# Three edits to a two-layer hybrid decoder trunk: a late weight part used later, two gated products on GpSimd, one low part first

## The chip, the cores and the metric

One core of one Trainium2 chip runs the whole program. The metric is the time of one execution in device microseconds (us); the figure of record is the median of the runs. Engines are named as the profile names them: PE is TensorE's matmul part and PEld its weight load, DVE is VectorE, ACT is ScalarE, POOL is GpSimd, SP is SyncE, whose queue issues nearly all DMAs.

## The reference, cut to what matters

Sequence 1024, model width 1024, everything float32. Layer 0 mixes with a gated linear recurrence, layer 1 with sliding-window attention; each layer then has a gated feed-forward block, and after each sub-layer stands a layer norm of `alpha * x + sublayer(x)`.

```python
def hgrn2_mixer(h, w_in, lower_bound, g_norm_w, w_out):      # layer 0
    q, f, i, g = jnp.split(h @ w_in, 4, axis=-1)
    ...
    o = hgrn2_chunkwise(jax.nn.silu(heads(q)), 1.0 - fg, heads(i), jnp.log(fg))
    o = o * lax.rsqrt(jnp.mean(jnp.square(o), -1, keepdims=True) + RMS_EPS)
    o = o * g_norm_w.astype(jnp.float32) * jax.nn.silu(heads(g))
    return o.reshape(B, S, D).astype(h.dtype) @ w_out
...
    o = jnp.einsum('bngrts,bnsgd->bntgrd', p, vv.astype(jnp.float32))   # layer 1
    o = o / jnp.moveaxis(denom, -1, 2)[..., None]
    return o.reshape(B, S, D).astype(h.dtype) @ w_out
...
def conv_ffn(h, w_in, conv_w, conv_b, w_out):                # both layers
    u = h @ w_in                                             # 1024 -> 2 x 2816
    u = lax.conv_general_dilated(u, ...) + conv_b            # causal, width 3
    a, b = jnp.split(u, 2, axis=-1)
    return (jax.nn.silu(a) * b) @ w_out
```

## The kernel before, in words

**Two parts of every number.** The large products are not done in plain float32. Each operand is kept as a high part (a cast to fp32r by ScalarE, the copy in `split`, line 221, or in `split_into`, line 176) and a low part (what is left, a VectorE subtraction in `low_part`, line 169). `mm3` (lines 193 to 197) then issues three matmuls: high by high (194), high by low (195) and low by high (196). So a block of activations (tile T) or of weights (HL, HT, TX) is ready for all three only when VectorE's subtraction is done, behind ScalarE's cast. `low_part` either issues the subtraction at once or, when it is given a list, puts a function there that issues it later.

**The order of the work.** Matmuls stand on PE in the order of the program text. In the recurrence and the attention the order on ACT, DVE and POOL is written out as well; there, a small planner (class `Order`) lets chains of work take turns at each `od.tick()`. In the feed-forward block (`Up`, `Down`) the order on ACT, DVE, POOL and SP is chosen by the compiler layer's scheduler, so one moved instruction can reorder its neighbours. Each engine carries out its own queue strictly in order, and so does SP's queue of DMA issues.

**Place 1, the beginning of layer 0's output projection (lines 1256 to 1274).** Seven of the eight heads' outputs are in T, and the last head's recurrence is still going on. Four accumulators of 128 tokens by 512 columns (`psmm`, one PSUM bank each) are begun: for each block `tb`, seven matmuls of T's high part by the weights' high part (`w` = 0), then seven by the weights' low part (`w` = 1), line 1263. After all four, line 1272 adds T's low part by the weights' high part. The weights `us[0]` to `us[6]` come from four weight units; the last unit holds `us[6]` (and `us[7]`), and its low part is the last one that VectorE makes. The planner sets matmuls of the last head's recurrence (`mm32`, line 200, and transposes, line 204) between them.

**Place 2, the up-projection's beginning, in both layers (`Up.run`, `Up.collect`).** A unit `fc` is 128 of the 2816 hidden columns, with both branches. Its product is put together from seven products of half size, `p` = 1 to 7, each 12 matmuls of 512 columns into one of eight PSUM banks (`psmm` and `psax`); `collect` adds the banks into rows of Y on DVE (lines 454 to 465). At `p` = 4 (first branch) and `p` = 3 (second branch) the width-3 convolution follows: one ACT operation (471) and two DVE operations (473); the first branch then has SiLU on ACT (476). The second branch's result is always in row 6 of Y; line 478 multiplies the two branches into row 4 or 5, and line 479 stores the row to DRAM (`gd`), to be read in the down-projection. Units 0 and 1 are made together and unit after unit from there. Beside this, `weight_sums` makes the next units' weights: sums and differences on DVE (425 to 428) and splits (ACT line 221, DVE line 169).

**Place 3, the attention's end (lines 1486 to 1517 and the lines after the loop).** Pairs of blocks (`bp`) of a head column `c` go through the stages of `attend`: scores and a copy of them (ACT 1410), bias and mask (POOL 1422), the row's extreme and exponential (DVE 1426, ACT 1429), normalisation (DVE 1432, 1433), transposes into a `psmm` bank (PE 204), products with a triangular mask (DVE 1441), and the product with the values into another `psmm` bank (`po`). For the last column, `c` = 7, the result is split straight out of PSUM into T (line 1457); its low part goes to the list `lows`, which `make_lows` empties from the front. In the loop's last turn the list holds already the low part of a move of finished columns from Y to T (`Y_to_T`). There are four `psmm` banks; at this point two of them hold accumulators of the output projection, and transposes and `po` share the other two.

Of the kernel before, what the change touches and what calls it, by code (L numbers as in the profile page):

```python
# [14 lines left out]
ALU = mybir.AluOpType  # L15

P = 128
# [90 lines left out]
def trunk(ctx: ExitStack, tc: tile.TileContext, a: dict, out: bass.AP):  # L108
# [240 lines left out]
    class Up:  # L349
# [97 lines left out]
        def collect(self, p, fc, ps):  # L447
            l, C = self.l, Y[:, 2 * (fc % 2):2 * (fc % 2) + 2, :]
            C11, C21, C12, C22 = C[:, 0, :512], C[:, 0, 512:], C[:, 1, :512], C[:, 1, 512:]
            if p == 1:  # L450
                nc.scalar.copy(C11, ps)
                nc.scalar.copy(C12, ps)
            elif p == 2:
                tt(C11, C11, ps, op=add)
            elif p == 6:
                tt(C12, C12, ps, op=add)
            elif p == 7:
                tt(C22, C12, ps, op=add)
            elif p == 4:
                tt(C21, C22, ps, op=add)  # L460
            elif p == 5:
                both = C[:, 1, :].rearrange("p (h n) -> p h n", h=2)
                tt(both, both, ps.unsqueeze(1).to_broadcast([P, 2, 512]), op=add)
            elif p == 3:
                tt(C12, C12, ps, op=add)
            if p in (4, 3):
                part = 0 if p == 4 else 1
                ci = fc + part * NF
                u, ca = C[:, part, :], Y[:, 4 + fc % 2, :]
                c = Y[:, 6, :] if part else ca  # L470
                nc.scalar.activation(c, u, AF.Identity, bias=cwt[:, l, 3, ci:ci + 1], scale=cwt[:, l, 2, ci:ci + 1])  # L471
                for sh in (1, 2):
                    nc.vector.scalar_tensor_tensor(c[:, sh:], u[:, :S - sh], cwt[:, l, 2 - sh, ci:ci + 1],  # L473
                                                   c[:, sh:], op0=ALU.mult, op1=ALU.add)
                if part == 0:
                    nc.scalar.activation(c, c, AF.Silu)
                else:
                    tt(ca, ca, c, op=ALU.mult)
                    nc.sync.dma_start(gd[:, fc, :], ca)

        def run(self, ready, down):
# [171 lines left out]
    with tc.tile_pool(name="t", bufs=1, reuse_waits="tile") as raws, hgrn_pool as hp:  # L653
# [538 lines left out]
        with tc.manual_schedule(engines={EN.PE, EN.SP, EN.Activation, EN.DVE, EN.Pool}):  # L1192
# [62 lines left out]
            moved.append(od.spawn(moves(NB // 2 - 1), 3.0))  # L1255
            us = out_us
            begun = []
            for tb in range(4):
                begun.append(psmm())
                ts = slice(tb * P, (tb + 1) * P)  # L1260
                for w in range(2):
                    for kc in range(KC - 1):
                        nc.tensor.matmul(begun[tb], T[:, 0, kc, ts], us[kc][:, w, :], start=w + kc == 0, stop=False)
                        od.t += 512 / 2365.0
                        od.tick()
            for tb in range(4):
                ts = slice(tb * P, (tb + 1) * P)
                movelows.sort(key=lambda m: m[0])
                while movelows and movelows[0][0] <= tb // 2:
                    lay_moved()  # L1270
                for kc in range(KC - 1):
                    nc.tensor.matmul(begun[tb], T[:, 1, kc, ts], us[kc][:, 0, :], start=False, stop=False)
                    od.t += 512 / 2365.0
                    od.tick()
            while values_done[0] < NH - 1:
                od.step(task)
            od.finish(moved)
# [30 lines left out]
    with (tc.tile_pool(name="ta", bufs=1, reuse_waits="tile") as raws,  # L1308
# [86 lines left out]
        def attend(c, bp, q):  # L1395
# [57 lines left out]
            if c < 7:  # L1453
                nc.scalar.copy(Y[:, c, bp * 256:(bp + 1) * 256], po[:, :256])
            else:
                ts = slice(bp * 256, (bp + 1) * 256)
                split(T[:, 0, c, ts], T[:, 1, c, ts], po[:, :256], lows)
            yield

        wo2 = a["swa_w_out"][0]  # L1460
# [151 lines left out]
```

## Time and profile before

| what | value |
|---|---|
| median of 3 runs (lowest to highest) | 2148.45 us (2147.89 to 2149.04) |
| the profiled execution's own time | 2147.93 us |
| its span, first to last instruction | 2146.1 us |
| PE busy / DVE busy / ACT busy / POOL busy in the span | 2130.6 / 1764.6 / 930.8 / 119.4 us |
| mean granted TensorE clock | 0.999 |

PE is busy for 99% of the span, so the table to read is that of PE's idle time: a list of some one-microsecond gaps, each with what ended it. Busy time of the other engines matters only where it makes one of those gaps. A row of the timeline gives start, duration, engine, line, operation, result `<-` sources, shape, how many were merged into it, and in square brackets the engine's idle time before it with what ended that.

### The profile page before, as it was taken

The numbers are of one execution on the slowest core, as the hardware profiler recorded it, in microseconds if no ns is written. First come the engines' busy times: TensorE is split into PE (matmuls) and PEld (weight loads), VectorE is DVE, ScalarE is ACT, GpSimd is POOL, SyncE is SP. The second block draws the span as 40 slices with busy tenths as digits, with TensorE's granted clock in tenths as the row PEclk, the third lists the DMA queues.
The fourth block names the chain that finished last, engine by engine and source line by source line (L and its number), as shares of the span: only waits on it lengthen the run. The fifth ranks groups of instructions, "written<-read, shape, count | busy, mean of one in ns | idle before, by whom it ended". The sixth has DMA issues, their size and how long they took to land.

```text
span 2146.1 us, 32133 instructions
## 1 busy us (share of the span) xinstructions
PE 2130.6 (99%) x12669; PEld 1780.8 (83%) x12669; DVE 1764.6 (82%) x2380; ACT 930.8 (43%) x1503; POOL 119.4 (6%) x143
## 2 busy tenths in 40 slices
PE   9999999999999999999999999999999999999998
PEld 8888888888888888888888888878888888888887
DVE  4777676677999999988978568969999899978986
ACT  4444444452454444444423356743544444444430
POOL 1000000000100000000001122311000000000002
PEclk9999999999999999999999999999999999999999
DMA  5655433214223222228754411133233222249762
GB/s 211 245 212 170 147 122 119 73 35 172 99 73 114 89 79 89 79 98 289 265 188 158 127 33 28 33 124 109 82 98 98 89 79 89 79 149 325 229 212 90
DMA packets 229838, 278.96 MB, mean 130 GB/s; under 512 B 29960, under 2 KB 158648, under 8 KB 226872
## 3 DMA queue, kind: packets, MB, share of 16 engines
q1 hardware_dynamic: 228736, 276.53, 38.5%
q8 instruction: 99, 1.62, 0.3%
q10 hardware_dynamic: 856, 0.37, 0.1%
q14 instruction: 51, 0.42, 0.1%
q0 software_dynamic: 96, 0.02, 0.0%
HBM read 213.94 MB, written 62.94 MB: 129 GB/s over the span
## 4 chain that ended last, share of the span: by engine, by line
PE 95%; DVE 3%; DMA 2%; issue 1%; ACT 0%; SPq 0%; DVEq 0%; ACTq 0%
PE psmm L194 17%; PE psmm L196 17%; PE psmm L195 16%; PE psax L194 9%; PE psax L195 9%; PE psax L196 9%; PE psmm L714 5%; PE psax L200 3%; PE psmm L715 3%; PE psmm L204 2%; PE psmm L200 1%; PE psax L1406 1%; PE psax L204 1%; DVE Y L473 1%; DVE T L169 1%
## 5 line engine op out<-in xcount | busy, mean ns | idle before, releaser
L194 PE MATMUL psmm<-T,HL 128*128 128x512 f32 x768 | 304.8, 397 | 0.0
L196 PE MATMUL psmm<-T,HL 128*128 128x512 f32 x768 | 299.4, 390 | 0.0
L195 PE MATMUL psmm<-T,HL 128*128 128x512 f32 x768 | 299.3, 390 | 0.0
L473 DVE SCALAR_TENSOR_TENSOR Y<-Y,cwt 128x1023 f32<-128x1023 f32 (+1 forms) x176 | 225.1, 1281 | 41.2 <-ACT Y L471 39.6
L221 ACT CAST HL<-rx 128x1024 fp32r<-128x1024 f32 (+1 forms) x151 | 151.7, 1008 | 208.8 <-PE psmm L195 45.3
L169 DVE TENSOR_TENSOR HL<-rx,HL 128x1024 fp32r<-128x1024 f32 (+1 forms) x151 | 174.7, 1162 | 15.3 <-ACT HL L221 14.9
L714 PE MATMUL psmm<-HL,T 128*128 128x512 f32 x496 | 176.9, 399 | 0.0
L196 PEld LDWEIGHTS psmm<-T,HL 128*128 128x128 f32 x768 | 144.2, 188 | 31.0
L194 PEld LDWEIGHTS psmm<-T,HL 128*128 128x128 f32 x768 | 144.3, 188 | 29.4 <-issue 0.4
L195 PEld LDWEIGHTS psmm<-T,HL 128*128 128x128 f32 x768 | 144.3, 188 | 27.8
L471 ACT ACTIVATE Y<-Y,cwt 128x1024 f32<-128x1024 f32 x88 | 108.8, 1238 | 98.8 <-DVE Y L460 93.8
L715 PE MATMUL psmm<-HL,T 128*128 128x256 f32 x496 | 138.9, 280 | 0.0
L194 PE MATMUL psax<-T,HL 128*128 128x512 f32 x352 | 137.3, 390 | 0.0
L196 PE MATMUL psax<-T,HL 128*128 128x512 f32 x352 | 137.0, 389 | 0.0
L195 PE MATMUL psax<-T,HL 128*128 128x512 f32 x352 | 137.0, 389 | 0.0
L243 POOL TENSOR_TENSOR rs<-rs,nhalf 128x1 f32<-128x1 f32 x32 | 45.6, 1424 | 1399.0 <-DVE rs L242 1399.0
L714 PEld LDWEIGHTS psmm<-HL,T 128*128 128x128 f32 x496 | 93.1, 188 | 21.1
L715 PEld LDWEIGHTS psmm<-HL,T 128*128 128x128 f32 x496 | 93.7, 189 | 0.4
L221 ACT CAST HT<-rx 128x1024 fp32r<-128x1024 f32 (+1 forms) x37 | 35.5, 960 | 107.8 <-DVE rx L427 75.9
L169 DVE TENSOR_TENSOR HL<-raw,HL 128x1024 fp32r<-128x1024 f32 x51 | 62.6, 1228 | 19.9 <-ACT HL L176 19.7
L196 PEld LDWEIGHTS psax<-T,HL 128*128 128x128 f32 x352 | 66.0, 188 | 13.7
L194 PEld LDWEIGHTS psax<-T,HL 128*128 128x128 f32 x352 | 66.1, 188 | 13.7
(314 smaller groups left out, 5237.0 us busy)
## 6 DMA issues: line engine op xcount, KB each, us to landing
rx<-in_ffn_w_in_dram SPq DMA_DIRECT2D x136, 256.0 KB, 3.1
rx<-gd SPq DMA_DIRECT2D x118, 256.0 KB, 3.6
Y<-in_ffn_w_out_dram SPq DMA_DIRECT2D x44, 512.0 KB, 6.1
bsd<-Y SPq DMA_DIRECT2D x22, 1024.0 KB, 4.8
gd<-Y SPq DMA_DIRECT2D x44, 512.0 KB, 2.6
rx<-in_ffn_w_out_dram SPq DMA_DIRECT2D x54, 256.0 KB, 4.8
R<-bsd SPq DMA_DIRECT2D x44, 256.0 KB, 4.9
Y<-in_ffn_w_in_dram SPq DMA_DIRECT2D x40, 256.0 KB, 2.9
```

The source lines that it names most:

```text
L169: make = lambda e: e.tensor_tensor(lo, src, hi.bitcast(F32), op=ALU.subtract)
L194: nc.tensor.matmul(ps, st(0), mv(0), start=start, stop=False)
L195: nc.tensor.matmul(ps, st(0), mv(1), start=False, stop=False)
L196: nc.tensor.matmul(ps, st(1), mv(0), start=False, stop=stop)
L200: nc.tensor.matmul(ps, lhsT, rhs, start=start, stop=stop, **kw)
L204: nc.tensor.transpose(ps, src, ident)
L221: nc.scalar.copy(hi, src)
L243: nc.gpsimd.tensor_tensor(rs, rs, nhalf, op=ALU.pow)
L471: nc.scalar.activation(c, u, AF.Identity, bias=cwt[:, l, 3, ci:ci + 1], scale=cwt[:, l, 2, ci:ci + 1])
L473: nc.vector.scalar_tensor_tensor(c[:, sh:], u[:, :S - sh], cwt[:, l, 2 - sh, ci:ci + 1], c[:, sh:], op0=ALU.mult, op1=ALU.add)
L714: nc.tensor.matmul(ps, T[:, 0, kc, ts], w[:, :, kc % 4, :], start=kc == 0, stop=False)
L715: nc.tensor.matmul(ps[:, :256], T[:, 1, kc, ts], w[:, 0, kc % 4, :], start=False, stop=kc == KC - 1)
```

## The change

Three edits:

1. In the output projection's beginning the matmuls of line 1263 and 1272 are issued by a helper, `out_pass`. The matmul of T's high part by the low part of `us[6]` (`w` = 1, `kc` = 6) is taken out of the first pass over the four accumulators and issued at the beginning of each accumulator's turn in the second pass. The 84 matmuls are the same; four of them come later.
2. In `Up.collect` the gated product (line 478) of units 0 and 1 is issued on GpSimd; those of units 2 to 21 stay on VectorE. This holds in both layers: four products move.
3. In `attend`, for the last column, the low part that is split out of PSUM is put at the front of `lows` and no longer at its end.

```diff
@@ -475,7 +475,7 @@
                 if part == 0:
                     nc.scalar.activation(c, c, AF.Silu)
                 else:
-                    tt(ca, ca, c, op=ALU.mult)
+                    (nc.gpsimd if fc < 2 else nc.vector).tensor_tensor(ca, ca, c, op=ALU.mult)
                     nc.sync.dma_start(gd[:, fc, :], ca)
 
         def run(self, ready, down):
@@ -1255,23 +1255,24 @@
             moved.append(od.spawn(moves(NB // 2 - 1), 3.0))
             us = out_us
             begun = []
+
+            def out_pass(ps, tb, x, w, kcs, start=False):
+                for kc in kcs:
+                    nc.tensor.matmul(ps, T[:, x, kc, tb * P:(tb + 1) * P], us[kc][:, w, :],
+                                     start=start and kc == 0, stop=False)
+                    od.t += 512 / 2365.0
+                    od.tick()
+
             for tb in range(4):
                 begun.append(psmm())
-                ts = slice(tb * P, (tb + 1) * P)
-                for w in range(2):
-                    for kc in range(KC - 1):
-                        nc.tensor.matmul(begun[tb], T[:, 0, kc, ts], us[kc][:, w, :], start=w + kc == 0, stop=False)
-                        od.t += 512 / 2365.0
-                        od.tick()
+                out_pass(begun[tb], tb, 0, 0, range(KC - 1), start=True)
+                out_pass(begun[tb], tb, 0, 1, range(KC - 2))
             for tb in range(4):
-                ts = slice(tb * P, (tb + 1) * P)
+                out_pass(begun[tb], tb, 0, 1, [KC - 2])
                 movelows.sort(key=lambda m: m[0])
                 while movelows and movelows[0][0] <= tb // 2:
                     lay_moved()
-                for kc in range(KC - 1):
-                    nc.tensor.matmul(begun[tb], T[:, 1, kc, ts], us[kc][:, 0, :], start=False, stop=False)
-                    od.t += 512 / 2365.0
-                    od.tick()
+                out_pass(begun[tb], tb, 1, 0, range(KC - 1))
             while values_done[0] < NH - 1:
                 od.step(task)
             od.finish(moved)
@@ -1454,7 +1455,9 @@
                 nc.scalar.copy(Y[:, c, bp * 256:(bp + 1) * 256], po[:, :256])
             else:
                 ts = slice(bp * 256, (bp + 1) * 256)
-                split(T[:, 0, c, ts], T[:, 1, c, ts], po[:, :256], lows)
+                first = []
+                split(T[:, 0, c, ts], T[:, 1, c, ts], po[:, :256], first)
+                lows[:0] = first
             yield
 
         wo2 = a["swa_w_out"][0]
```

In the built program the first edit leaves every other engine's order as it was; the recurrence's matmuls stand after the same number of output-projection matmuls (18, 11, 14, and then the rest). The third edit exchanges two neighbouring DVE instructions. The second lets the scheduler reorder DVE, ACT and SP over the rest of each up-projection. In layer 1, DVE's queue from unit 2's first bank sum (line 454) on stands like this (operation by line; W is the weight block that PE needs first, the low part from row 7 of Y, a result `HL<-Y`):

```
before: 454 478 456 169(HT) 169(HL) 473 458 473 460 478 463 473 465 473 427 473 428 473 169(W)
after:  454 169(HT) 456 427 473 458 473 428 460 169(W) 169(HL) 473 463 473 465 ...
```

In layer 0 the queue after the same point is `454 428 456 169(W) 473 458 473 460 169(HL) 463 ...`, where before it had `454 478 456 428 458 473 460 473 169(HL) 478 473 463 473 465 169(W)`.

## The prediction, made before the changed kernel ran

> **What bounds the kernel now.** I read the page first, then PE's waits, then the busy time by stretch, then the timeline around each gap.
>
> ```profile
> span 2146.1 us, 32133 instructions
> PE 2130.6 (99%) x12669; PEld 1780.8 (83%) x12669; DVE 1764.6 (82%) x2380; ACT 930.8 (43%) x1503; POOL 119.4 (6%) x143
> ```
>
> PE is idle for only 2146.1 - 2130.6 = 15.5 us. Since the change neither adds nor removes a matmul, this is all that a change of order can win, and only the part that lies at the three places. The waits of PE name what ended its larger gaps:
>
> ```profile
> PE psmm L204 <- DVE T L169: 1.3, 1, 1.3
> PE psmm L1263 <- DVE HL L169: 1.2, 1, 1.2
> ...
> PE psmm L196 <- DVE HL L169: 1.0, 1, 1.0
> ```
>
> Three waits, one at each place, all for a low part from VectorE: 1.3 us at a transpose of the attention (place 3), 1.2 us at the output projection (place 1), 1.0 us at a weight block (place 2). The stretches show where the rest of the idle time lies (first columns: the stretch, its length, PE's busy time; the third engine column is DVE, the fifth POOL):
>
> ```profile
> 455.00:500.00 45.00, 43.84 (x344) 36.86 (x344) 26.59 (x46) 17.69 (x42) 1.83 (x2) 1.00 0.36 136
> ...
> 600.00:1000.00 400.00, 400.00 (x1766) 331.20 (x1766) 362.43 (x397) 179.08 (x194) 0.00 (x0) 1.00 0.32 104
> ...
> 1415.00:1440.00 25.00, 23.58 (x144) 18.79 (x142) 12.26 (x20) 7.67 (x23) 1.29 (x1) 1.00 0.64 213
> ...
> 1520.00:1600.00 80.00, 78.97 (x349) 65.08 (x348) 76.19 (x89) 37.91 (x42) 0.00 (x0) 1.00 0.28 86
> ```
>
> The three stretches hold 1.16 + 1.42 + 1.03 us of PE's idle time. Layer 0's feed-forward block, which the second edit also touches, holds none: there an edit can only lose. The granted clock is 1.00 in all four, so a gap closed is time saved at the same speed.
>
> **Edit 1: the late weight part.** Rows of PE, DVE and ACT around the gap:
>
> ```profile
> 458.68 3.25 PE L1263 MATMUL psmm<-HL,T 128*128 128x512 f32 x13
> 463.08 1.42 PE L1263 MATMUL psmm<-HL,T 128*128 128x512 f32 x5 [1.16 <-DVE HL L169]
> ...
> 466.30 2.77 PE L1263 MATMUL psmm<-HL,T 128*128 128x512 f32 x11
> 468.91 1.27 PE L200 MATMUL psax<-VG,kd 128*128 128x128 f32 x10
> ...
> 461.81 1.22 DVE L169 TENSOR_TENSOR HL<-raw,HL 128x1024 fp32r<-128x1024 f32 x1
> ...
> 465.57 0.58 ACT L958 COPY A<-psax 64x512 f32<-64x512 f32 x1
> 466.64 1.02 ACT L1045 COPY kd<-psax 128x1024 f32<-128x1024 f32 x1 [0.49 <-PE psax L204]
> ```
>
> The first accumulator runs 13 matmuls (7 high, then 6 low) up to 461.93; the fourteenth is the one by the low part of `us[6]`, which VectorE has ready at 461.81 + 1.22 = 463.03. PE idles 1.16 us. After the edit the fourteenth matmul on PE is the next accumulator's first, whose operands have been read once already, and the moved ones come after 52 matmuls, long behind 463.03. So the gap goes, and nothing is added: the same 84 matmuls.
>
> What is late next? The recurrence's steps stand after the same counts of matmuls, so they come 1.16 us earlier. The first that might be late is the product with `kd` at 468.91, then wanted at 467.75. `kd` is the ACT copy of line 1045, itself released by PE's transposes (they move along); ahead of it stands line 958, which cannot come much before 465.5, because ACT is busy there. So the copy starts about 466.1, ends at 467.1, and 0.6 us are left. I take **-1.16 us**; the bounds are -0.7 (if the copy is 0.5 us later than this) and -1.16.
>
> **Edit 3: the low part in PSUM first.**
>
> ```profile
> 1417.19 1.11 PE L200 MATMUL psmm<-W,Vt 128*64 128x128 f32 x16
> 1417.34 0.69 DVE L1433 TENSOR_TENSOR X<-X,dn 128x512 f32<-128x512 f32 x1
> 1417.94 1.22 DVE L169 TENSOR_TENSOR T<-Y,T 128x1024 fp32r<-128x1024 f32 x1
> 1419.08 0.42 DVE L169 TENSOR_TENSOR T<-psmm,T 128x256 fp32r<-128x256 f32 x1
> 1419.41 0.68 DVE L1426 TENSOR_REDUCE nm<-X 128x4 f32<-128x516 f32 x1
> ...
> 1419.64 0.63 PE L204 MATMUL psmm<-ident,X 128*128 128x128 f32 x4 [1.34 <-DVE T L169]
> ```
>
> PE's transposes need two things: X, which is ready at 1417.34 + 0.69 = 1418.03, and a `psmm` bank. Of the four, two hold accumulators, and the one that is due holds a `po` until its low part has been read, at 1419.08 + 0.42 = 1419.50. That small subtraction waits behind the 1.22 us one from Y. Exchanged, it takes 1417.94 to 1418.36, and the transposes follow 0.14 us later, as in the row, at 1418.50: **-1.14 us**. PE's earlier work ends at 1418.30, so 0.20 us of the 1.34 stays. The part from Y ends at 1419.50 where it ended at 1419.16; it feeds token blocks 4 and up, which PE reaches only after the accumulators of blocks 2 and 3. VectorE's next instruction (1426) keeps its start, so the softmax of the last pair stays where it was while PE comes 1.14 us earlier; PE wants it only at the next transposes, some 6 us on. I see no wait there. The first residual load into Y goes out 0.3 us later on SP; it is wanted tens of microseconds later. Bounds: 0 (if X or another bank were the true reason) and -1.34.
>
> **Edit 2: four products on GpSimd.** First the gap and VectorE's queue up to it:
>
> ```profile
> 1554.32 0.68 DVE L454 TENSOR_TENSOR Y<-Y,psmm 128x512 f32<-128x512 f32 x1
> 1554.92 1.22 DVE L478 TENSOR_TENSOR Y<-Y 128x1024 f32<-128x1024 f32 x1
> ...
> 1556.17 1.25 ACT L471 ACTIVATE Y<-Y,cwt 128x1024 f32<-128x1024 f32 x1 [1.09 <-DVE Y L478]
> ...
> 1558.39 1.28 DVE L473 SCALAR_TENSOR_TENSOR Y<-Y,cwt 128x1023 f32<-128x1023 f32 x1
> ...
> 1570.82 1.22 DVE L169 TENSOR_TENSOR HL<-Y,HL 128x1024 fp32r<-128x1024 f32 x1
> ...
> 1570.67 0.39 PE L195 MATMUL psmm<-TX,HL 128*128 128x512 f32 x1
> 1572.09 0.50 PE L196 MATMUL psmm<-TX,HL 128*128 128x512 f32 x1 [1.03 <-DVE HL L169]
> ...
> 1574.49 0.39 PE L194 MATMUL psax<-TX,HL 128*128 128x512 f32 x1
> ```
>
> PE asks for the low part (W) at 1570.67 + 0.39 = 1571.06; VectorE delivers it at 1572.04. VectorE is the late one: 76.19 of 80 us busy. Now GpSimd's price. No row shows this multiplication on GpSimd, but two rows lie near, and one shows what it does to VectorE:
>
> ```profile
> 6.88 2.38 POOL L169 TENSOR_TENSOR HL<-raw,HL 128x1024 fp32r<-128x1024 f32 x1 [2.04 <-DVE HL L730]
> ...
> 8.60 1.74 DVE L169 TENSOR_TENSOR HL<-raw,HL 128x1024 fp32r<-128x1024 f32 x1 [0.22 <-ACT HL L176]
> ...
> 1415.75 1.29 DVE L1441 TENSOR_TENSOR W<-psmm,tri 128x512 f32<-128x512 f32 x2
> ...
> 1415.85 1.29 POOL L1422 TENSOR_TENSOR X<-X,bf 128x512 f32<-128x512 f32 x1 [3.60 <-DVE X L1414]
> ...
> L1422 POOL TENSOR_TENSOR X<-X,bf 128x512 f32<-128x512 f32 x32 | 41.4, 1293 | 97.4 <-ACT X L1429 41.9 <-DVE X L1414 36.6 <-ACT Y L1454 17.6
> ```
>
> A subtraction of the same size takes 2.38 us, and half the size 1.29, twice which is 2.59. I take 2.4 us, twice VectorE's 1.22. In the second row VectorE's subtraction with both sources in SBUF takes 1.74 instead of 1.22 us while GpSimd works until 9.26: 0.52 us lost in 0.66 us of overlap, so VectorE stands for 0.79 of the time. Operations with a PSUM source lose nothing: two of them beside GpSimd took 1.29 us together, the 0.60 and 0.68 of undisturbed ones.
>
> Now the new queue, with the rows' durations (a 1.22 to 1.28 operation is followed by the next after 1.14 to 1.20, a 0.68 one after 0.60). 454 starts at 1554.32 as before; 169(HT), 456 and 427 end the run at 1556.7. GpSimd's first product starts when 473 has ended, 1554.5, and ends at 1556.9. ACT's next 471 writes row 6 of Y, which that product reads, so it waits for it: 1557.0, and VectorE's 473 follows 1.2 us later, at 1558.2 (before: 1558.39). VectorE is idle from 1556.7 to 1558.2, which takes in what it loses beside the first product. Then 473, 458, 473, 428, 460 take 1.2 + 0.6 + 1.2 + 0.6 + 0.6 = 4.2, so W starts at 1562.4 and ends at 1563.6; beside the second product (1561.3 to 1563.7) it loses up to 1.0. At 1564.6 W is 6.5 us ahead of PE's 1571.06. The gap is closed: **-1.03 us**. Most of this comes from the order (463, two 473 and 465 now stand behind W), not from the 1.14 us of each product.
>
> What is pushed back: 465 frees a `psax` bank for PE's product at 1574.49, now wanted at 1573.46. Behind W stand 169(HL), 473, 463, 473: 1.14 + 1.20 + 1.13 + 1.20, so 465 runs from about 1569.3 to 1570.0 with the loss counted: 3.5 us to spare. The write of the product to `gd` leaves SP 0.5 us later, and the weight loads queued behind it need W's row of Y, free some 8 us sooner. In layer 0 the same account holds with W moved up even further; VectorE's saving of 2 x 1.14 and its loss of at most 2 x 0.79 x 2.4 = 3.8 come to 1.5 us net, which I charge at nothing: with eight banks PE asks for one again eight products later, 96 matmuls 0.24 us apart (3.25 less the last one's 0.39, over 12 steps, in the rows of edit 1), some 23 us. Bounds of the second edit: -1.03, and + some microseconds if GpSimd is much slower (rival 1).
>
> The Trainium skill, GPSIMD Engine Reference, section "Engine selection", sends an elementwise multiplication to VectorE, GpSimd being about twice as slow with two inputs, and its section "Key points" says that GpSimd shares its SBUF interfaces with VectorE, in contention with VectorE's instructions that have two SBUF inputs. This case's rows agree with both: 2.38 beside 1.22 us, and 1.74 in place of 1.22. By that rule alone the edit would give VectorE work rather than take it; rival 1 is what that would cost.
>
> **Sum.** -1.16 - 1.14 - 1.03 = -3.33 us. The profiled execution took 2147.93 us, 1.8 above its span (what lies before and after the first and last instruction), so 2144.6 for it. The median of the runs stands 0.52 above the profiled one: 2148.45 - 3.33 = **2145.1 us**, 0.15% faster. About 0.2% (4.3 us) is what a measurement of this kernel can tell from no change; so the forecast counts as no change, because the whole idle time at the three places, 1.16 + 1.42 + 1.03 = 3.6 us, is less than that.
>
> **Rivals.**
> 1. *GpSimd and VectorE hold each other up* (slower). If the products stretch to d us each, W starts at 1560.0 + d and VectorE loses 0.79 x (d - 1) beside the second; 465 then ends near 1566.5 + d + 0.79 x (d - 1) and is late for 1573.46 from d = 4.3 on, 1.8 times the row. Against: the row's GpSimd subtraction kept its pace while VectorE gave way. At three times the row, d = 7.1, 465 is 4.9 us late, in both layers if layer 0 has the same room: 2 x 4.9 - 3.33 = +6.5 us, **2154.9**.
> 2. *The first gap only moves*: ACT's `kd` copy is late, or the recurrence's steps do not come earlier; half of 1.16 is lost: **2145.7**.
> 3. *The third gap moves to the next late item* on VectorE, which is still busy to 95%: -2.3 us, **2146.2**.
> 4. *The third edit does not do what it says*, since the transposes wait for something else than the bank: -2.2, **2146.3**. The waits put it down to that very subtraction, and 0.14 us after it is the pace; little speaks for this.
>
> **Chances.** Forecast 0.66; rival 1 with milder forms of it 0.12 (half of that beyond 2152.75); rival 2 0.08; rival 3 0.07; rival 4 0.04; 0.03 for nothing gained at all. The runs before lie within 0.6 us of their median, so the forecast's time may read 2144.3 to 2145.9. The range, 2144.0 to 2147.8, takes in the forecast, rivals 2 to 4 and the lighter half of rival 1. Faster than 2144.15: 0.10, from the forecast's lower edge. Slower than 2152.75: 0.07. Within: 0.83.
>
> **What would show it.** Right: the waits of PE have no row for line 1261, the attention's transposes wait 0.2 us, no L196 waits for HL in the up-projection; POOL is busy about 9.6 us more, in rows of 2.4 us; PE's idle time is some 12.2 us. Wrong: new waits of PE for DVE at lines 454 to 465 or for ACT at 451 and 452 in either up-projection; POOL rows of line 478 of 5 us or more; a wait for `kd` near 468; PE idle between 600 and 1000, where there was none.

## The result, and the profile after

The changed kernel takes **2144.69 us** (median of 19 runs, 2143.30 to 2147.05) against 2148.48 us for the kernel before (median of 19 runs, 2146.57 to 2151.18): a ratio of 0.9983, 95% interval 0.9976 to 0.9989. That is 3.8 us or 0.17%, forecast were 3.3. The interval does not reach 1, so there is a gain, of 2.4 to 5.2 us. The profiled execution took 2144.58 us with a span of 2142.7 (before: 2147.93 and 2146.1).

From the page, and from the list of PE's waits (waiter `<-` what ended it: us in total, times, longest):

```profile
span 2142.7 us, 32143 instructions
PE 2130.8 (99%) x12669; PEld 1781.1 (83%) x12669; DVE 1765.0 (82%) x2376; ACT 927.5 (43%) x1503; POOL 128.9 (6%) x147
```

```profile
...
PE psmm L204 <- DVE Y L255: 0.7, 1, 0.7
PE psax L194 <- DVE Y L594: 0.6, 1, 0.6
...
PE psmm L204 <- DVE T L169: 0.2, 1, 0.2
PE psmm L204 <- ACT Y L378: 0.2, 1, 0.2
```

PE's idle time fell from 15.5 to 2142.7 - 2130.8 = 11.9 us. The rows for line 1263 (now 1261) and for L196 are gone, the attention's transposes wait 0.2 us in place of 1.3. But there are two rows that before had not: L204 for DVE L255 and for ACT L378, 0.7 and 0.2 us. And one row of before is missing that no edit touches, PE's wait of 1.0 us for the first load of x. The same stretches as in the prediction, and the one with the new waits (length, PE, PEld, DVE, ACT, POOL):

```profile
455.00:500.00 45.00, 45.00 (x350) 38.11 (x348) 28.12 (x47) 17.79 (x42) 1.83 (x2) 1.00 0.39 141
600.00:1000.00 400.00, 400.00 (x1766) 331.32 (x1765) 361.64 (x392) 176.21 (x193) 4.80 (x2) 1.00 0.33 106
1415.00:1440.00 25.00, 24.79 (x145) 20.00 (x142) 9.98 (x16) 6.04 (x14) 0.00 (x0) 1.00 0.71 216
1440.00:1520.00 80.00, 79.13 (x381) 65.67 (x380) 78.62 (x122) 32.00 (x48) 11.86 (x8) 1.00 0.33 113
1520.00:1600.00 80.00, 80.00 (x355) 66.24 (x354) 76.18 (x85) 36.35 (x41) 5.10 (x2) 1.00 0.29 90
```

The three places now show 0, 0.21 and 0 us of idle time; layer 0's feed-forward block still shows none; between 1440 and 1520, where before PE was never idle, it is idle for 0.87 us.

The timeline at the three places, in the order of edits 1, 3 and 2:

```profile
457.65 4.37 PE L1261 MATMUL psmm<-HL,T 128*128 128x512 f32 x18
461.96 1.09 PE L200 MATMUL psax<-kd 128*32 128x64 f32 x32
...
464.98 1.00 ACT L1045 COPY kd<-psax 128x1024 f32<-128x1024 f32 x1
466.43 1.72 PE L200 MATMUL psax<-VG,kd 128*128 128x128 f32 x14
...
1415.41 0.42 DVE L169 TENSOR_TENSOR T<-psmm,T 128x256 fp32r<-128x256 f32 x1
1415.74 1.22 DVE L169 TENSOR_TENSOR T<-Y,T 128x1024 fp32r<-128x1024 f32 x1
1415.97 0.63 PE L204 MATMUL psmm<-ident,X 128*128 128x128 f32 x4 [0.21 <-DVE T L169]
...
1553.32 2.40 POOL L478 TENSOR_TENSOR Y<-Y 128x1024 f32<-128x1024 f32 x1 [43.75 <-DVE Y L473]
1553.66 2.60 DVE L169 TENSOR_TENSOR HT<-Y,HT 128x512 fp32r<-128x512 f32 x1
1560.62 2.71 POOL L478 TENSOR_TENSOR Y<-Y 128x1024 f32<-128x1024 f32 x1 [4.91 <-DVE Y L473]
1561.57 2.83 DVE L169 TENSOR_TENSOR HL<-Y,HL 128x1024 fp32r<-128x1024 f32 x1
1568.98 0.67 DVE L465 TENSOR_TENSOR Y<-Y,psax 128x512 f32<-128x512 f32 x1
...
1568.66 0.39 PE L196 MATMUL psmm<-TX,HL 128*128 128x512 f32 x1
1570.92 0.39 PE L194 MATMUL psax<-TX,HL 128*128 128x512 f32 x1
```

The reader is to see three things. The `kd` copy ends at 465.98, 0.45 us ahead of the product that needs it. The exchange of the two subtractions leaves 0.21 us of the 1.34. And beside GpSimd's products (2.40 and 2.71 us) VectorE's subtractions with both sources in SBUF last 2.60 and 2.83 us, where alone they last 0.69 and 1.22. W still ends at 1564.40, 4.3 us ahead of its first use.

**A wait costs more than its idle time.** At place 1 the kernel before has, behind the same 18 matmuls (from 458.68 on, rows in the prediction):

```profile
464.44 1.09 PE L200 MATMUL psax<-kd 128*32 128x64 f32 x32
```

That is 5.76 us from the first of the 18 to the next step, and 4.31 after (457.65 to 461.96): 1.45 us less, though the idle time that went is 1.16. The rows say why. Back to back, these matmuls start 0.23 us apart, but a row lasts 0.39, so the idle time of a row begins 0.16 us after the next start was due; and in the kernel before, the second matmul behind the wait started 0.34 us after the first, 0.11 late. So the time that a place gained is better read from the starts of the same matmul in the two executions:

| stretch | PE's starts, after less before |
|---|---|
| from the beginning up to place 1 | -1.02 (it scatters, see the experiments) |
| place 1 | -1.45 |
| place 3 | -1.14 |
| layer 1's first layer norm | +1.41 |
| place 2 | -1.33 |
| all the rest | +0.08 |
| whole execution | -3.45 |

The three places gave 3.92 us, not 3.33, and the layer norm took back 1.41.

The new waits, and the same place before (the transposes by line 204 of layer 1's first layer norm, and the VectorE instruction, line 255, that ends a token block's norm):

```profile
1491.26 1.28 DVE L255 SCALAR_TENSOR_TENSOR Y<-Y,rs,rx 128x1024 f32<-128x1024 f32 x1
1492.69 1.16 PE L204 MATMUL psmm<-ident,Y 128*128 128x128 f32 x8 [0.71 <-DVE Y L255]
1499.93 0.66 PE L204 MATMUL psmm<-ident,Y 128*128 128x128 f32 x4 [0.15 <-ACT Y L378]
```

```profile
1493.20 1.28 DVE L255 SCALAR_TENSOR_TENSOR Y<-Y,rs,rx 128x1024 f32<-128x1024 f32 x1
1495.48 1.03 PE L204 MATMUL psmm<-ident,Y 128*128 128x128 f32 x8
```

Before (second fence) line 255 ended at 1494.48 and PE came at 1495.48: a **margin** of 1.00 us, which no wait shows. After, PE would have come at 1491.98, and line 255 ended at 1492.54; PE started 0.15 us behind that end. Where PE waits, the margin is written below as the wait with a minus sign, here -0.71.

### The profile page after: what moved, and what is told of

Read it like the earlier page. It is cut to its first block, busy times and chain, and to the rows that moved or that the text cites. A ratio compares the mean times of both kernels' runs of the same rounds, so it can differ in the third digit from the quotient of the medians.

```text
span 2142.7 us, 32143 instructions
## 1 busy us (share of the span) xinstructions
PE 2130.8 (99%) x12669; PEld 1781.1 (83%) x12669; DVE 1765.0 (82%) x2376; ACT 927.5 (43%) x1503; POOL 128.9 (6%) x147
## 5 line engine op out<-in xcount | busy, mean ns | idle before, releaser
L194 PE MATMUL psmm<-T,HL 128*128 128x512 f32 x768 | 304.8, 397 | 0.0
L196 PE MATMUL psmm<-T,HL 128*128 128x512 f32 x768 | 299.5, 390 | 0.0
L196 PEld LDWEIGHTS psmm<-T,HL 128*128 128x128 f32 x768 | 144.1, 188 | 30.8
L194 PEld LDWEIGHTS psmm<-T,HL 128*128 128x128 f32 x768 | 144.3, 188 | 29.5 <-issue 0.4
L194 PE MATMUL psax<-T,HL 128*128 128x512 f32 x352 | 137.3, 390 | 0.0
L196 PE MATMUL psax<-T,HL 128*128 128x512 f32 x352 | 137.0, 389 | 0.0
L196 PEld LDWEIGHTS psax<-T,HL 128*128 128x128 f32 x352 | 66.2, 188 | 13.8
L194 PEld LDWEIGHTS psax<-T,HL 128*128 128x128 f32 x352 | 66.1, 188 | 13.6
```

The costliest lines, as they stand in the source:

```text
L194: nc.tensor.matmul(ps, st(0), mv(0), start=start, stop=False)
L196: nc.tensor.matmul(ps, st(1), mv(0), start=False, stop=stop)
```

## The experiments

Twelve more kernels ran, one of them the changed kernel again, in three groups; each group shared the runs of the kernel before on its chip. A difference of two medians is uncertain by up to 2 us here (the intervals reach some 0.0009 to either side), so for smaller differences the waits and starts of PE in the profile decide. Line numbers of kernels with added lines are 1 to 4 higher.

### Each edit by itself

The first four kernels leave out edits of the diff: edit 1 alone, edit 2 alone, edit 3 alone, edits 1 and 3.

> The first edit alone (the late weight part's four matmuls moved behind the first pass; products on VectorE, low part in PSUM last, as before). Theory: the three places are independent and only shift PE in time. The 1.16 us gap at the output projection's beginning is gone and nothing of it comes back, so -1.2 us against the kernel before; PE keeps the waits of 1.3 us at an attention transpose and of 1.0 us at L196 in the second up-projection. PE reaches layer 1's layer norm 1.2 us earlier, and there the slack is about 2 us, so no wait of L204 for DVE L255. Rival A: the gap only moves (kd, or the recurrence), half or all of it is lost: -0.6 to 0 us, with a new PE wait between 460 and 600 us. Rival B: any earlier PE is late-weight-bound in layer 1's output projection: a wait of about 0.5 us for DVE L255 appears here already, and the total is -0.7.

> The second edit alone (four products on GpSimd). Theory: -1.0 us, all in the second up-projection: no L196 waits for HL there, POOL rows of line 478 of 2.4 to 2.7 us, nothing new in layer 0, and no wait in layer 1's layer norm, which stands ahead of the second up-projection. Rival A: the layer norm's new wait of 0.7 us, seen with all three edits, comes from the GpSimd products of layer 0 (a changed DMA order behind them): then it appears here, and the total is -0.3. Rival B: without the earlier PE of the other edits the scheduler's queue of VectorE stands differently against PE, and W is late all the same: 0.

> The third edit alone (the low part in PSUM ahead of the one from Y). Theory: the wait of the transposes falls from 1.34 to 0.2 us, -1.1 us at that place; PE is then 1.1 us earlier in layer 1's output projection, within the slack of about 2 us against the late output weights, so at most 0.2 us of it comes back: -1.0 us in all. Rival A: what comes back is the third edit's own doing (the low part from Y, now 0.34 us later, delays VectorE's queue and the layer norm): then the whole 0.7 to 0.9 us wait for DVE L255 appears here, and the total is -0.3. Rival B: the wait does not go: 0.

> The first and third edit together, all products on VectorE. Theory: PE is 2.3 us earlier in layer 1's output projection, the late weights' chain is not, and the layer norm's transposes wait 0.7 to 0.9 us as with all three edits; L196 in the second up-projection still waits for HL, but less than 1.0 us, since PE gets there only some 1.5 us earlier while VectorE's chain moves with it: -1.2 to -1.6 us in all, the difference to all three edits about 1.0 us. Rival A: the layer norm's wait comes from the GpSimd products: no such wait here, -2.3 us. Rival B: the sum of the two edits is kept in full because the chain from the late weights moves along: -2.3 us, no wait, and what was seen with all three edits was a chance of that one profiled execution.

| kernel | median us (before in the same group: 2148.14) | ratio, 95% | PE idle in the profile | wait at place 1 / 3 / 2 | margin at the layer norm |
|---|---|---|---|---|---|
| edit 1 | 2146.22 | 0.9992 (0.9983 to 1.0000) | 13.6 | 0 / 1.34 / 0.81 | 1.27 |
| edit 2 | 2145.98 | 0.9991 (0.9983 to 1.0000) | 14.3 | 1.22 / 1.34 / 0 | 0.31 |
| edit 3 | 2146.99 | 0.9995 (0.9986 to 1.0004) | 13.8 | 1.15 / 0.20 / 0.81 | 1.03 |
| edits 1 and 3 | 2144.93 | 0.9987 (0.9978 to 0.9995) | 12.0 | 0 / 0.21 / 0.96 | 0.82 |

The medians alone settle nothing: they differ from before by 1.9, 2.2, 1.2 and 3.2 us, with 1.2, 1.0, 1.0 and 1.2 to 1.6 expected, and the three single edits add up to more than all three together gained. By the waits the first three theories hold at the places: each edit closes its own gap, leaves the other two within 0.22 us, and at the place itself nothing of it comes back. By PE's starts, edit 1 gains 1.45 us in both kernels that have it, edit 3 1.14 in both, edit 2 1.32. One part of the second theory did not hold: at the layer norm no wait for line 255 came, but the margin fell to 0.31, and a later wait of line 204 there, 0.13 us of idle time, cost PE 0.38 us by its starts. The theory for the fourth **fell**. I had taken the new wait for the price of PE's earlier coming: the late output weights of layer 1 land behind 4 MB of residuals, so VectorE's chain would stay where it is while PE comes 2.3 us earlier. With edits 1 and 3 PE does come earlier, and the margin is 0.82, against 1.00 before. The chain moved along.

The table also shows what scatters from one execution to the next. The wait for the first load of x near 10 us is 1.01, 0.58, 0 and 0.74 us in before and the first three of the table, and 0 in the fourth, in identical code. A wait of the down-projection's first product (L194 for DVE L594, near 1034 or 1980) reads 0.47 before and between 0 and 1.4 us at a time in the others (2.5 with all products on GpSimd). So one profiled span says little to within 1 us.

### Order or offload, and the late loads

Two kernels have edits 1 and 3 with all products on VectorE, and give the making of the next weights a higher priority in the scheduler, which moves W ahead by order alone:

```diff
-            self.weights(2)
+            with urgent():
+                self.weights(2)
```

The second of them also puts the loads of layer 1's late output weights earlier in the program:

```diff
-        for tb in range(NB):
+        for tb in range(4):
             nc.sync.dma_start(Y[:, tb, :], resid(tb))
...
                     out_late(late, rows, tb, ff.TX)
+                    nc.sync.dma_start(Y[:, tb + 4, :], resid(tb + 4))
```

In the built program this is milder than meant: eight of the sixteen weight loads stand ahead of the last two residual loads, four between them.

> The first and third edit, all products on VectorE, and in the up-projection the making of unit 2's and 3's weights given to the scheduler as urgent, so that W is issued earlier by order alone. Theory (the second edit's gain is the order's, not the offload's): no L196 waits for HL in either up-projection, W ends well ahead of PE's call, VectorE's W and HT rows last 1.2 and 0.7 us, POOL is not busy there; -1.0 us against the two orders alone (at that place PE waited 0.96 us), the same time as all three edits within 0.5 us, -3.3 against the kernel before. Rival A: without the products off its hands VectorE can't bring W and the bank sums in time: a wait at L196, or at L194/L195 for a bank (DVE 454 to 465), of 0.5 to 1.0 us stays. Rival B: the reorder pushes another item late in the up-projection of layer 0, where there was no idle time: 0 to +2 us there.

> The run before, and the sixteen loads of the late output weights in layer 1 issued ahead of the last four of the eight residual loads. Theory: the layer norm's transposes there were late because the split of the late weights waits for their DMA behind 4 MB of residuals, which the third edit starts 1.46 us later against PE. So the first split starts some 5 us earlier, VectorE's L255 ends more than 1.5 us ahead of the transposes (0.8 us in the run of the two orders), and no wait of L204 for DVE L255 or ACT L378: -3.3 us against the kernel before, with less spread. Rival A: the margin at the layer norm is set by the later loads of the up-projection's weights (or by VectorE's own work), which these loads do not release: margin as before, about 0.8 us. Rival B: the residuals of blocks 4 to 7, now last, come late: a new wait at L326 or for the output projection's sums, 0 to +3 us.

**Measured**: 2144.42 us for the order alone (ratio 0.9981, 0.9973 to 0.9990) and 2144.15 with the loads (0.9981, 0.9972 to 0.9990), before 2148.58. The gap at L196 is gone in both without GpSimd. From the timeline of the order alone:

```profile
1567.50 1.24 DVE L169 TENSOR_TENSOR HL<-Y,HL 128x1024 fp32r<-128x1024 f32 x1
1568.80 0.50 PE L196 MATMUL psmm<-TX,HL 128*128 128x512 f32 x1
```

W ends at 1568.74 and PE uses it at 1568.80: just in time, not "well ahead" as I had expected. By PE's starts the order alone gains 1.16 us at place 2, and 1.33 with the loads moved, where edit 2 gains 1.33. So the second edit's gain is the order's; the GpSimd kernel's order has 4.3 us in hand, this one none. The margin at the layer norm is about 0 with the order alone (line 255 ends at 1492.66, PE starts at 1492.81) and **2.40** with the loads moved (1491.85 and 1494.25), with the first split of the late weights 17.9 us behind the transposes of place 3 in place of 21.7 (3.8 us sooner, some 5 expected). That part of the theory holds, rival A falls.

### What a product on GpSimd costs

Two kernels take all three edits and more of the suspected cost: the four products done twice on GpSimd (its units 0 and 1 then hold silu(a) x b x b, not what the reference computes), and all 44 products there.

```diff
+                    if fc < 2:
+                        nc.gpsimd.tensor_tensor(ca, ca, c, op=ALU.mult)
                     (nc.gpsimd if fc < 2 else nc.vector).tensor_tensor(ca, ca, c, op=ALU.mult)
```

```diff
-                    (nc.gpsimd if fc < 2 else nc.vector).tensor_tensor(ca, ca, c, op=ALU.mult)
+                    nc.gpsimd.tensor_tensor(ca, ca, c, op=ALU.mult)
```

> All three edits, and GpSimd multiplies units 0 and 1 by the second branch twice, so that d is 4.8 us in place of 2.4 (the output's units 0 and 1 are changed by it: silu(a)*b*b). Theory, from the rows of all three edits: 465 ended at 1569.65 and its bank was wanted at 1570.92, 1.27 us to spare. ACT's 471 is now 2.4 us later, and with it 473 and the queue behind; VectorE, which stands for 0.9 of the overlap with its instructions from SBUF, loses 1 to 3 us more: 465 is 2 to 4 us late, a wait of PE at L194 for psax of 2 to 4 us in layer 1, and something like it in layer 0: +2 to +6 us against all three edits, +0 to +3 against the kernel before. Rival A, the prediction's own account (late from d = 4.3 on): 465 late by 0.8 us in layer 1, +0.8 to +1.7. Rival B: VectorE's idle time before 473 takes it all in: 0.

> All three edits, and all 22 gated products of each layer on GpSimd (44 in place of 4). Theory: a product takes 2.4 to 2.7 us on GpSimd, saves VectorE 1.14 us and costs it 0.9 us for each microsecond of overlap with an instruction that has both sources in SBUF; ACT's 471 of the next unit waits for the product (row 6 of Y), so each unit's convolution starts at least 1.2 us later. VectorE was 95% busy in the up-projections, so it becomes late for PE's banks in most units: new waits of PE for DVE at 454 to 465, some 0.2 to 0.7 us a unit, +8 to +30 us. Rival: the contention falls mostly into instructions with a PSUM source, which lose nothing, and VectorE gains 1.14 us a unit: DVE's busy time falls by 40 x 1.1 = 45 us and the time stays as with all three edits.

**Measured**, one run each: 2149.98 us for the products twice, 2157.73 for all of them (before 2148.58). PE's timeline of the first (only rows with a wait that the edit brought):

```profile
628.31 0.50 PE L194 MATMUL psax<-TX,HL 128*128 128x512 f32 x1 [1.15 <-DVE Y L465]
1571.90 0.50 PE L196 MATMUL psmm<-TX,HL 128*128 128x512 f32 x1 [0.60 <-DVE HL L169]
1576.02 0.50 PE L194 MATMUL psax<-TX,HL 128*128 128x512 f32 x1 [1.55 <-DVE Y L465]
```

With 2.4 us more for each product, W is late again in layer 1 (0.60 us), and line 465 is late in both layers, by 0.60 + 1.55 us in layer 1, counted from when PE would have come, and by 1.15 in layer 0: 3.3 us in place of the 0.8 to 1.7 of the prediction's account. All products, from the groups by line (count, busy time, mean ns):

```profile
L169 DVE TENSOR_TENSOR HL<-rx,HL 128x1024 fp32r<-128x1024 f32 x135 | 232.5, 1723 | 15.6 <-ACT HL L221 15.6
...
L478 POOL TENSOR_TENSOR Y<-Y 128x1024 f32<-128x1024 f32 x44 | 108.6, 2469 | 759.8 <-DVE Y L473 741.5 <-ACT HL L221 18.3
```

From the page, and the stretch of layer 0's feed-forward block:

```profile
PE 2137.4 (99%) x12669; PEld 1779.2 (83%) x12669; DVE 1789.9 (83%) x2336; ACT 919.1 (43%) x1503; POOL 227.4 (11%) x187
```

```profile
600.00:1000.00 400.00, 397.97 (x1744) 325.60 (x1744) 371.73 (x372) 172.49 (x194) 54.74 (x22) 1.00 0.31 99
```

VectorE is rid of 40 more products, 40 x 1.22 = 48.8 us, and is busy 1789.9 - 1765.0 = 24.9 us *more*: a product on GpSimd costs it (48.8 + 24.9) / 40 = **1.84 us, for the 1.22 that it saves**. The low parts HL from rx alone went from a mean of 1.22 us (1218 ns, 135 of them, before) to 1.72. The rival falls; the loss of 13 us is in the lower half of what the theory gave. Only half of the 13 us is idle time in the profile: in the stretch PE shows 2.0 us of idle time, but did 22 matmuls fewer than after, and those are 5 us at 0.23 us each. The other 3 us went in delays of at most 0.14 us each, by PE's starts, which leave no idle time, since a row of 0.39 us covers them.

### How VectorE loses time beside GpSimd

Two kernels cut each of the four products in two and in four instructions:

```diff
-                    (nc.gpsimd if fc < 2 else nc.vector).tensor_tensor(ca, ca, c, op=ALU.mult)
+                    if fc < 2:
+                        for k in range(0, S, 512):      # 256 for quarters
+                            nc.gpsimd.tensor_tensor(ca[:, k:k + 512], ca[:, k:k + 512], c[:, k:k + 512], op=ALU.mult)
+                    else:
+                        tt(ca, ca, c, op=ALU.mult)
```

> All three edits, each of the four products on GpSimd cut in two instructions of 512 columns (1.29 us each by the row of line 1422). The question is how VectorE loses time beside GpSimd. Theory 1, one at a time: an instruction of VectorE with both sources in SBUF does nothing until GpSimd's instruction has ended (in the runs so far it ended 0.54 us after it where its own time is 0.69, and 1.07 us after it where that is 1.22, for overlaps from 1.7 to 2.3 us). Then with halves VectorE gets in between them: the low part HT beside the first product lasts about 1.5 us in place of 2.60, W at most 2.4 in place of 2.83, and GpSimd's second half is the one that waits (a row of about 1.8 us). Theory 2, a share: VectorE runs at a tenth of its speed as long as GpSimd works; HT stays at 2.5 to 2.6 us. Time: within 0.5 us of all three edits by both.

> The same with four instructions of 256 columns, about 0.74 us each (1.29 at 512 and 2.40 at 1024 columns make 0.18 plus 2.17 for 1024). Theory 1, one at a time: HT lasts at most 0.54 + 0.74 = 1.3 us and W at most 1.07 + 0.74 = 1.8, whichever of GpSimd's pieces they meet; GpSimd's rows are stretched instead, the four from 3.0 to some 4 us in sum. Theory 2, a share: HT 2.5, W 2.8, and GpSimd's pieces 0.74 each. Time: within 0.7 us of all three edits by both.

**Measured**, one run each: 2145.40 and 2145.18 us. HT and W with halves, then with quarters, and with quarters what came of it (start, duration; rows picked; x2 and x4 are the pieces):

```profile
1553.16 3.00 POOL L480 TENSOR_TENSOR Y<-Y 128x512 f32<-128x512 f32 x2 [43.44 <-DVE Y L473]
1553.50 1.50 DVE L169 TENSOR_TENSOR HT<-Y,HT 128x512 fp32r<-128x512 f32 x1
1560.72 3.81 POOL L480 TENSOR_TENSOR Y<-Y 128x512 f32<-128x512 f32 x2 [4.56 <-DVE Y L473]
1561.66 1.73 DVE L169 TENSOR_TENSOR HL<-Y,HL 128x1024 fp32r<-128x1024 f32 x1
```

```profile
1551.55 0.94 DVE L169 TENSOR_TENSOR HT<-Y,HT 128x512 fp32r<-128x512 f32 x1
1559.55 6.28 POOL L480 TENSOR_TENSOR Y<-Y 128x256 f32<-128x256 f32 x4 [4.56 <-DVE Y L473]
1560.49 1.22 DVE L169 TENSOR_TENSOR HL<-Y,HL 128x1024 fp32r<-128x1024 f32 x1
1570.63 0.62 ACT L221 CAST HL<-Y 128x512 fp32r<-128x512 f32 x1 [8.42 <-DMA Y<-in_ffn_w_in_dram]
1574.35 0.50 PE L194 MATMUL psax<-T,HL 128*128 128x512 f32 x1 [1.73 <-ACT Y L452]
```

HT lasts 2.60, 1.50, 0.94 us beside whole, halved and quartered products, W 2.83, 1.73, 1.22. A share of the time would have left them as they were, so theory 2 falls: the two engines work **one at a time**, instruction by instruction. (The expectation's "2.17 for 1024" should read 2.22; its 0.74 us stands.) With quarters it is GpSimd that waits (3.8 and 6.28 us for a product), and that is paid elsewhere: the store of the product to `gd` holds SP's queue until the product ends at 1565.83, so the weight load behind it goes out at 1566.29, though its row of Y was free at 1561.71 (in the changed kernel the load went out at 1564.43); ACT waits 8.42 us for it, and PE 1.73 us for ACT. With halves the subtraction behind W lasts 2.30 us in place of 1.21, so the two together take as long as with whole products. Cutting the product moves the wait, it does not take it away.

The Trainium skill, SBUF — State Buffer, section "SBUF: two separate sides", says the same: VectorE, with two SBUF inputs, and GpSimd take a shared port pair by a lock for a whole instruction, and the other "fully blocks". By that rule HT and W end one own duration after GpSimd's product; the trace agrees but for a constant 0.14 to 0.15 us (they end 0.54 and 1.07 us behind it, 0.69 and 1.22 alone).

### The changed kernel once more, and with the loads moved

> The changed kernel once more, to see whether the layer norm's wait belongs to it. Theory: the weight load that VectorE's queue waits for near 1464 lands 4.3 to 4.5 us after its issue in the kernels with products on GpSimd and 3.6 to 3.9 in those without; PE comes 2.3 us earlier; so the transposes near 1492 wait 0.4 to 0.9 us for DVE L255 again. Rival: the 0.71 us was a chance of that one execution, the margin is about +0.3 us, no wait. Time -3.3 to -3.7 us against the kernel before.

> All three edits, and the sixteen loads of layer 1's late output weights ahead of the last four residual loads. Theory: with the orders alone this moved VectorE's L255 from 0.0 to 2.4 us ahead of the transposes; here it moves it from 0.7 us behind to some 1.7 us ahead, the waits of L204 for DVE L255 and ACT L378 go, -0.9 us against the changed kernel on the same chip. Rival: the weight load that lands late after the products on GpSimd sets the margin by itself, whatever the late weights do: a wait of 0.3 to 0.7 us stays, -0.2 us.

**Measured**: 2144.53 us (ratio 0.9984, 0.9974 to 0.9993) and **2143.62 us** (0.9980, 0.9971 to 0.9989), before 2148.10. The layer norm in the first and in the second:

```profile
1491.52 1.28 DVE L255 SCALAR_TENSOR_TENSOR Y<-Y,rs,rx 128x1024 f32<-128x1024 f32 x1
1492.95 1.16 PE L204 MATMUL psmm<-ident,Y 128*128 128x128 f32 x8 [0.23 <-DVE Y L255]
```

```profile
1489.30 1.28 DVE L255 SCALAR_TENSOR_TENSOR Y<-Y,rs,rx 128x1024 f32<-128x1024 f32 x1
1492.68 1.03 PE L204 MATMUL psmm<-ident,Y 128*128 128x128 f32 x8
```

The wait is there again, with 0.23 in place of 0.71 us (by PE's starts the layer norm takes back 0.94 in place of 1.41): less than the theory's 0.4 to 0.9, and the margin is below zero again, against the rival's +0.3. With the loads moved the margin is 2.10 us and the wait is gone; that kernel has the lowest median of all, 0.9 us below the changed kernel beside it, as forecast, though the two intervals overlap and the medians can't tell it from the order alone.

**What stays open.** The margins at the layer norm were 1.00 before; 1.27, 1.03 and 0.82 with edit 1, edit 3 and both; 0.31, -0.71 and -0.23 with edit 2 in whole products, -0.29 with products twice, about 0 with all 44, but 0.59 and 1.18 with halves and quarters, and about 0 with the order alone. The last thing VectorE's chain waits for there is a weight load, issued near 1460. ACT's split of it began 3.65 to 3.91 us after its issue in the six kernels without products on GpSimd (before among them), 4.09 to 4.47 in the six with whole ones, and 3.8 with halves and quarters. That is some 0.5 us of the difference, in a load that in the changed kernel comes 840 us after layer 0's last product on GpSimd; why was not found.

VectorE's rows show where the rest went: from its first subtraction for the late weights (1439.82) to the end of line 255 the changed kernel takes 1.27 us longer than edits 1 and 3 do, and 1.16 of this are two waits, 0.90 in place of 0.18 for that load's split and 0.44 in place of 0 for line 243, the norm's small step on GpSimd, which lasts 2.06 us there and 1.46 with edits 1 and 3. The order alone has that second wait twice, without any product on GpSimd, and by PE's starts loses 0.62 us at this norm.

And scatter can be as large: at layer 0's layer norm, which stands ahead of every product on GpSimd, PE's starts move by -0.23 to +0.92 us against before in kernels whose VectorE, ScalarE and GpSimd have the same order there (-0.06 in the changed kernel, +0.92 with products twice). Shown is that the margin depends on when the late weights land, since moving their loads raised it by over 2 us twice; how much of its loss is edit 2's doing and how much is scatter is not.

## Why the prediction was right, and where not

The time (2145.1 forecast, 2144.69 measured), the three mechanisms and the verdict held: 0.17% is within the 0.2% that were to count as no change. None of the four rivals' losses came about, though rival 1's condition did: GpSimd and VectorE do hold each other up, only not for long enough to make PE late. That the sum came so close is partly luck. Two of its terms were too small, by 0.6 us together, and what the layer norm takes back, 0.9 to 1.4 us in the two profiles of the changed kernel, was put at nothing; these errors have opposite signs, and a median here is not sharp enough to show what is left of them.

- **Edit 1, -1.16**: the mechanism is right, the size too small. The wait's idle time went in full, but PE gained 1.45 us, since the row of a wait leaves out 0.29 of what it cost. `kd` had 0.45 us to spare where I had 0.6.
- **Edit 3, -1.14**: right at its place, to 0.01 us (1.34 to 0.21; by PE's starts 1.14). Here a wait stays, before and after, and so does its surcharge.
- **Edit 2, -1.03**: the reason is right, order alone closes the gap; the size was too small again, 1.33 us by PE's starts. The sign "POOL busy 9.6 us more" reads 9.5.
- **"VectorE stands for 0.79 of the time"**: this step failed. The row it came from (0.52 us lost in 0.66 of overlap) shows the same constant 0.14 us as all later ones: nothing is shared. So the offload gives VectorE no relief at all: it is busy 1765.0 us after and 1764.6 before, though four products, 4.9 us, have left it.
- **"6.5 us ahead" and "3.5 us to spare"**: both too large, by 2.2 us. W is 4.3 us ahead, and 465 ended at 1569.65 with its bank wanted at 1570.92: 1.27 us. About half of the 2.2 is PE's: the forecast let PE and VectorE keep their distance, but PE's call for W came 2.40 us earlier than before (1571.06 to 1568.66) and VectorE's queue, by its instruction 454, only 1.26 (1554.32 to 1553.06). The other half is W's: it lasted 2.83 us where 2.2 were allowed, and began 0.43 us later after 454 than forecast. The decisive product length of rival 1, put at 4.3 us, is therefore lower. At 4.8 us the doubled products were late by 3.3 us in all; in layer 1 line 465 came 2.15 us late for 2.4 us more per product, from 1.27 to spare, so it was late from about 2.4 + 2.4 x 1.27 / 3.42 = 3.3 us on (an estimate, by a straight line between the two runs). GpSimd's 2.4 us was much closer to costing time than the forecast said.
- **"The first residual load ... is wanted tens of microseconds later"** and **"I see no wait there"**: the step was looked at for the softmax only. What counts is what the residuals delay on SP's queue, the late weights, and where VectorE's chain from them meets PE: a margin of 1.00 us, which no list of waits shows, and which ended at -0.71 and -0.23. It gave back 1.41 us in the profiled execution (0.87 of it idle time). The cause first put forward for it, PE's earlier coming alone, did not hold.
- **The start**: the profiled execution of before had 1.01 us of PE's wait for x, which comes and goes. It hid the 0.87 us of idle time at the layer norm: that PE's idle time of 11.9 us looks like the 12.2 forecast is luck.

## What to carry to other kernels

Where the bounding engine is 99% busy, a gap's own row gives the place and the least that closing it gains (the starts of the same matmul in both executions give the rest), and the margins of the places behind it give what comes back: measure them as the consumer's start less the producer's end, also where no wait is shown. An offload to GpSimd that leaves VectorE's neighbours with two SBUF sources is no offload; look whether the new order alone does the same. A queue of loads is an order too: here, putting the loads that a chain waits for ahead of those it does not raised its margin by over 2 us, twice.

## What the runs showed of the hardware

- In the rows read here, a VectorE instruction with both sources in SBUF and a GpSimd product never ran together; whichever came second waited for the whole instruction, less 0.14 us. VectorE's instructions with a PSUM source lost nothing (454: 0.68 us beside the first product, 460: 0.67 beside the second).
- A GpSimd product of 128x1024 took 2.40 us, and 2.71 where a VectorE subtraction held it up; with pieces of 256 columns VectorE's instructions went in between, and one product took 6.28 us.
- The split of the same load at the same point began 3.65 to 4.47 us after the load's issue, in two executions of the same program 4.09 and 4.46; margins below a microsecond behind a DMA are not safe.
- PE's busy time can hold waiting: back to back, matmuls of 512 columns started 0.23 us apart while a row lasts 0.39, so a delay of up to 0.16 us shows no idle time, and a wait of 1.16 us cost 1.45 (397.97 us busy in a stretch of 400, with 22 of 1766 matmuls fewer done).
